# The feed-forward part of a decoder step: 18 seven-product tiles that add in PSUM, with down products between their blocks

## The chip, the cores and the metric

The kernel runs on one core of a Trainium2 chip. The metric is the device time of one execution in microseconds, from the runs shown below. Engines are called PE or TensorE (matmuls; PEld is its weight load), DVE or VectorE, ACT or ScalarE, POOL or GpSimd, and SP (the queue that issues most of the loads).

## The reference

One layer of a decoder trunk, for 512 prompt tokens and 8 sample tokens that share the weights (520 columns in all), D = 1024, feed-forward width 2816, all float32. The edit concerns its last part:

```
h2 = RMSNorm(x) * (1 + scale2) + shift2
gu, up = split(h2 @ w_ffn_in)            # 1024 -> 2 x 2816
x = x + gate2 * ((silu(gu) * up) @ w_ffn_out)   # 2816 -> 1024
y = RMSNorm(x)
```

Ahead of it stand adaLN, the input projection, an RG-LRU branch, an attention branch (prompt, and sample tokens with a paged cache) and the projection of their sum; none of that is touched.

## The kernel before, in words

Activations are kept transposed: features on the 128 partitions, the 520 tokens along the free axis, in two halves of 260 (`L_`, `R_`). Products of float32 are made of three fast ones: each operand is split into a high part (`hi`, an ACT cast) and a low rest (`lo`, a VectorE difference), and the matmuls are hi x hi, lo x hi, hi x lo. So one product of a 128x128 weight tile with half the tokens is three matmuls of 128x260. A weight tile of the common kind is split by L226 (ACT, `whi`) and L228 (VectorE, `wlo`).

The feed-forward part works through 22 tiles `jt` of 128 features. A tile is made in one of two ways.

- A plain tile (`ffn_tile`): gate (`fig`) and up (`fiu`) each need 8 weight tiles x 2 halves x 3 = 48 matmuls, 96 in all.
- A seven-product tile (`fast_tile`, the tiles in `FAST`): gate and up are taken as one 2x2 block product, of weight halves by token halves, with seven block products instead of eight (A11, A12, S2, S3, S1, A22, S4); a block is 4 weight tiles x 3 = 12 matmuls, 84 in all. The weight blocks S1 to S4 are sums and differences of raw weights that POOL makes (`ws`, L241 to L244). Each block's weights are split by L248 (ACT) and L249 (VectorE) into a `wb` tile. Each block product has a PSUM bank of its own. VectorE adds the seven into four results in SBUF (L1565, seven sums), ACT takes Silu of the gate, VectorE multiplies (L1568) and the result is split into `ach` (ACT, L1435) and `acl` (VectorE, L1436).

Tiles 0 and 1 are done by halves in a loop of their own, 2 and 3 are plain. The 22 tiles stand in four sections (`SECT`: 6, 6, 5, 5 tiles). At the end of a section its down products follow: for each of the 8 output tiles a `product` over the section's tiles (`fo`), and `residual` adds it to `x`, times the gate, on VectorE (L1392 for the left half; L1396, L1399 and L1400 for the right half and its 8 sample columns). The last section's down products go by halves (`by_halves`), since the sum of squares for the final norm is made beside them, on POOL for the first outputs; the outputs of the left half follow on POOL (L1518) during the right half.

Order: each engine works through its own queue. Weights are handled as a list of `units`, one for each stretch of matmuls; `begin` starts a unit, asks for the loads of units up to 22 us ahead (`load_chunks`, on SP) and for the splits of units up to 11 us ahead (`split_upto`). The split weights live in two rings of three buffers (`whi`, `wlo`); a block uses one buffer of either, a common weight tile one of each. Raw weights live in `wraw`, two buffers of 1 MB; `pg` is another pool of seven buffers. PSUM has eight banks, and 60 buffers in `heap` hold everything of 520 columns. The lines above are those of the profile.

Of the kernel before, what the change touches and what calls it, by code (L numbers as in the profile page):

```python
# [8 lines left out]
F32 = mybir.dt.float32  # L9
# [10 lines left out]
NS = 8  # L20
# [3 lines left out]
FF = 2816  # L24
# [40 lines left out]
def kernel(ctx, tc, xT, par, gates, b_f, cst, cse, own, cache_k, cache_v, cache_lf, pt,  # L65
# [76 lines left out]
    SECT = ((0, 6), (6, 12), (12, 17), (17, 22))  # L142
    PLAIN = 2
    CH_FI = len(chunks)
    for j0, j1 in SECT:
        for jt in range(j0, j1):
            chunks.append(cols(w_fi, 128 * jt, 128) + cols(w_fi, FF + 128 * jt, 128))
        for i in range(0, KT, 2):
            chunks.append(cols(w_fo, 128 * i, 256, 128 * j0, j1 - j0))


    FAST = (4, 5, 6, 7, 9, 10, 12, 13, 15, 16, 17, 18, 20)
    BLOCKS = ("A11", "A12", "S2", "S3", "S1", "A22", "S4")
    units = []
    for c, parts in enumerate(chunks):
        nk = parts[0][2]
        if parts[0][0] is w_fi and parts[0][3] // 128 in FAST:
            units += [(c, name, 4) for name in BLOCKS]
            continue
        for o in range(0, sum(p[4] for p in parts), 128):  # L160
            units.append((c, o, nk))
# [43 lines left out]
    def split_upto(n):  # L205
        while state["split"] < len(units) and state["split"] <= n:
# [5 lines left out]
            if isinstance(o, str):  # L212
                splits[m] = split_block(raw, o)
                continue
# [20 lines left out]
    def split_block(raw, name):  # L235
# [9 lines left out]
        src = blocks[name]  # L245
# [1144 lines left out]
    def residual(f, ps, gate, j):  # L1390
# [4 lines left out]
        n = NP - HALF  # L1395
        dve.scalar_tensor_tensor(x[f][:, HALF:NP], ps[:, :n], mod[:, gate, f, 0:1], x[f][:, HALF:NP],  # L1396
                                 ALU.mult, ALU.add)
        t = small("rs", 128, NS)
        dve.tensor_tensor(t, ps[:, n:HALF], mod[:, gate, f, 1:9], ALU.mult)  # L1399
# [163 lines left out]
    def fast_tile(jt):  # L1563
        t, v, w, out = slot("sw"), slot("v"), slot("w"), pair_out()
        add = lambda o_, a_, b_: dve.tensor_tensor(o_, b_, a_, ALU.add)  # L1565

        def close(j, part):
            dve.tensor_tensor(t[:, part], t[:, part], w[:, part], ALU.mult)  # L1568
            split_part(out, t[:, part], part)

        for name in BLOCKS:
            n = begin()
            b = bank(f"fi{jt}_{name}")[:, :HALF]
            hi, lo = splits[n]
            for k in range(4):
                ah, al = h2_block(name, k)
                for m, (wt, at) in enumerate(((hi, ah), (lo, ah), (hi, al))):
                    state["mm"] = pe.matmul(b, lhsT=wt[k], rhs=at, start=k == 0 and m == 0, stop=k == 3 and m == 2)  # L1578
            if name == "A11":
                act.copy(w[:, R_], b)  # L1580
            elif name == "A12":
                add(t[:, L_], w[:, R_], b)
                act.activation(t[:, L_], t[:, L_], AF.Silu)
            elif name == "S2":
                add(v[:, L_], w[:, R_], b)
            elif name == "S3":
                add(w[:, L_], v[:, L_], b)
            elif name == "S1":
                add(w[:, R_], w[:, L_], b)
                add(v[:, R_], v[:, L_], b)  # L1590
            elif name == "A22":
                add(w[:, L_], w[:, L_], b)
                close(0, L_)
            else:
                add(t[:, R_], v[:, R_], b)
                act.activation(t[:, R_], t[:, R_], AF.Silu)
                close(1, R_)
            run_later(n)
        return out

    for sec, (j0, j1) in enumerate(SECT):
        ac = []
        if j0 == 0:
            ts = [slot("sw") for _ in range(PLAIN)]
            ready = []
            u = state["n"]
            for j in range(2):
                for m in range(2 * PLAIN):
                    if j == 0:
                        begin(u + 3)  # L1610
                    b = bank(f"fi{m}_{j}")
                    half_product(u + m, j, h2, b)
                    ready.append((times_up if m % 2 else swish, b, ts[m // 2], j))
                    if j == 0 and m == 0:
                        rstd_half("r2", ss2, r2, 1)
                    if j or m:
                        for fn, *args in ready:
                            fn(*args)
                        ready.clear()
                    if j == 0 and m == 0:  # L1620
                        h2_half(1)
                    first = u + 2 * PLAIN
                    if j == 0:
                        load_chunks(units[first + m][0])
                    elif m:
                        split_upto(first + m - 1)
            for t in ts:
                out = pair_out()
                split_part(out, t)
                ac.append(out)  # L1630
        for jt in range(max(j0, PLAIN), j1):
            if jt == PLAIN:
                for k in range(4):
                    h2_blocks(k)
                defer(0, lambda: split_blocks(0))
# [71 lines left out]
```

## Time and profile before

| | |
|---|---|
| time, median of 3 runs | 1046.94 us (1045.0 to 1053.59) |
| profiled execution | 1044.21 us, span of its instructions 1042.3 us |
| PE busy | 998.9 us (96%), 8054 instructions |
| DVE busy | 777.5 us (75%) |
| ACT busy | 533.2 us (51%) |
| POOL busy | 304.0 us (29%) |
| granted TensorE clock, mean | 0.991 |
| chain that ended last | PE 70%, DVE 12%, DMA 7%, ACT 5% |

The feed-forward part fills the time from about 660 us to the end. A busy share is a mean over all stages; the chain of work that ended last, read in order of time, says for each stage which engine the others wait for. Rows of the group view give line, engine, operation, out<-in and shapes, then busy us, mean ns of one, and the idle time of the engine before them with what ended it.

### The profile page before, as it was taken

Reading aid. Unit: us, or ns where it says so; the run is one execution under the profiler, and the core shown is the slowest. Engines: PE = TensorE matmul, PEld = TensorE weight load, DVE = VectorE, ACT = ScalarE, POOL = GpSimd, SP = SyncE. Lnnn points to the kernel's source line nnn. Section 1 sums busy time; section 2 is a strip of 40 time slices with the busy share of each in tenths; the row PEclk is TensorE's granted clock in tenths of the full one; section 3 lists DMA queues with packets and bytes.
Section 4 is the critical chain, followed back from the end, with each engine's and each line's share of the span. In section 5 each row is a group of like instructions: output and inputs, shape, how many; then the busy total and the mean of one; then the engine's idle time right before and its main releaser. Section 6 shows DMA issues by size and latency. Waiting matters only on the chain.

```text
span 1042.3 us, 21246 instructions
## 1 busy us (share of the span) xinstructions
PE 998.9 (96%) x8054; PEld 925.8 (89%) x8054; DVE 777.5 (75%) x1370; ACT 533.2 (51%) x1072; POOL 304.0 (29%) x411
## 2 busy tenths in 40 slices
PE   4999999999999999999999999899999999999993
PEld 1888899999898988878888989899999999999993
DVE  5447999988989978886665546778589558869663
ACT  4523665857671467767793234555244324524451
POOL 0224411112133235654500003472224033223113
PEclk9999999999999999999999999999999999999997
DMA  9898987787889999996766863132343234143212
GB/s 326 295 306 289 300 281 216 262 253 270 263 253 309 321 326 284 303 274 213 263 230 209 282 226 82 41 82 75 100 111 83 91 111 121 54 128 102 75 52 83
DMA packets 165353, 206.97 MB, mean 199 GB/s; under 512 B 9842, under 2 KB 126082, under 8 KB 165186
## 3 DMA queue, kind: packets, MB, share of 16 engines
q1 hardware_dynamic: 148530, 152.52, 47.2%
q0 software_dynamic: 13040, 46.67, 13.5%
q10 hardware_dynamic: 3680, 6.42, 1.7%
q8 instruction: 63, 1.03, 0.4%
q14 instruction: 40, 0.33, 0.1%
HBM read 192.49 MB, written 13.09 MB: 197 GB/s over the span
## 4 chain that ended last, share of the span: by engine, by line
PE 70%; DVE 12%; DMA 7%; ACT 5%; issue 4%; POOL 1%; SPq 0%; POOLq 0%; DVEq 0%; ACTq 0%
PE fo L281 11%; PE fi_S L1578 7%; PE fi_A L1578 5%; PE pb L281 4%; PE gb L281 4%; PE fig L281 4%; PE fiu L281 4%; PE ga L281 3%; PE k L281 3%; PE wo L281 3%; PE v L281 3%; DVE wlo L228 2%; PE gr L281 2%; PE xr L281 2%; DMA wraw<-in_w_in_dram 2%
## 5 line engine op out<-in xcount | busy, mean ns | idle before, releaser
L226 ACT CAST whi<-wraw 128x1024 fp32r<-128x1024 f32 (+2 forms) x113 | 111.4, 987 | 186.1 <-PE fo L281 45.0
L228 DVE TENSOR_TENSOR wlo<-wraw,whi 128x1024 fp32r<-128x1024 f32 (+2 forms) x113 | 137.3, 1216 | 48.6 <-ACT whi L226 40.9
L281 PE MATMUL fo<-ach,whi 128*128 128x260 f32 x302 | 85.6, 283 | 0.0
L281 PE MATMUL fo<-ach,wlo 128*128 128x260 f32 x302 | 85.2, 282 | 0.0
L281 PE MATMUL fo<-acl,whi 128*128 128x260 f32 x302 | 85.0, 282 | 0.0
L658 POOL DMA_DIRECT2D pg<-in_cache_k_dram x74 | 39.4, 533 | 142.4 <-DVE S L707 70.5
L241 POOL TENSOR_TENSOR ws<-wraw 128x512 f32<-128x512 f32 x13 | 20.0, 1538 | 193.5 <-DMA wraw<-in_w_fi_dram 188.7
L706 DVE TENSOR_TENSOR pg<-pg,qb 128x1024 f32<-128x1024 f32 x48 | 58.0, 1227 | 2.4 <-DMA pg<-in_cache_k_dram 2.4
L707 DVE TENSOR_REDUCE S<-pg 128x16 f32<-128x1024 f32 x48 | 57.0, 1207 | 0.1
L281 PEld LDWEIGHTS fo<-ach,whi 128*128 128x128 f32 x302 | 56.8, 188 | 0.2
L281 PEld LDWEIGHTS fo<-ach,wlo 128*128 128x128 f32 x302 | 56.8, 188 | 0.0
L281 PEld LDWEIGHTS fo<-acl,whi 128*128 128x128 f32 x302 | 56.8, 188 | 0.0
L1191 POOL TENSOR_SCALAR p<-p,mu 128x128 f32<-128x128 f32 (+3 forms) x28 | 35.9, 1293 | 48.2 <-DVE mu L1187 31.6
L249 DVE TENSOR_TENSOR wb<-ws,wb 128x512 fp32r<-128x512 f32 x52 | 45.8, 891 | 4.2 <-ACT wb L248 4.1
L373 POOL TENSOR_TENSOR ss<-ss,sq 128x260 f32<-128x260 f32 x18 | 13.7, 761 | 111.3 <-PE ada L344 58.9
L248 ACT CAST wb<-ws 128x512 fp32r<-128x512 f32 x52 | 31.5, 619 | 26.2 <-PE fi_S L1578 8.6
L1185 ACT ACTIVATE p<-p,mu 128x128 f32<-128x128 f32 (+3 forms) x64 | 35.3, 552 | 15.8 <-DVE mu L1184 15.5
L248 ACT CAST wb<-wraw 128x512 fp32r<-128x512 f32 x39 | 23.9, 620 | 34.7 <-PE fo L281 18.1
L1396 DVE SCALAR_TENSOR_TENSOR x<-fo,mod,x 128x252 f32<-128x252 f32 x32 | 15.2, 477 | 32.4 <-PE fo L281 32.4
L1435 ACT CAST ach<-sw 128x260 fp32r<-128x260 f32 (+1 forms) x42 | 17.6, 419 | 41.5 <-DVE sw L1477 22.3
L281 PE MATMUL v<-hh,whi 128*128 128x260 f32 x128 | 37.3, 291 | 1.1 <-DVE pl L1205 1.1
L1578 PE MATMUL fi_S<-twh,wb 128*128 128x260 f32 x208 | 38.1, 282 | 0.0
(435 smaller groups left out, 4065.7 us busy)
## 6 DMA issues: line engine op xcount, KB each, us to landing
araw<-in_ada_w_dram SPq DMA_DIRECT2D x48, 512.0 KB, 6.2
wraw<-in_w_fi_dram SPq DMA_DIRECT2D x44, 512.0 KB, 5.2
pg<-in_cache_k_dram POOLq DMA_DIRECT2D x42, 512.0 KB, 6.2
pg<-in_cache_v_dram SPq DMA_DIRECT2D x42, 512.0 KB, 5.5
wraw<-in_w_in_dram SPq DMA_DIRECT2D x34, 512.0 KB, 7.7
wraw<-in_w_in_dram SPq DMA_DIRECT2D x11, 1024.0 KB, 10.3
pg<-in_cache_v_dram POOLq DMA_DIRECT2D x22, 512.0 KB, 6.4
pg<-in_cache_k_dram POOLq DMA_DIRECT2D x32, 256.0 KB, 5.7
```

Source lines behind the costliest of these rows:

```text
L226: state["act"] = act.copy(hi[:, :k1 - k0], src)
L228: state["last"] = dve.tensor_tensor(lo[:, :k1 - k0], src, hi[:, :k1 - k0].bitcast(F32), ALU.subtract)
L241: pool.tensor_tensor(s1, a21, a22, ALU.add)
L248: state["act"] = act.copy(t[:, :4], src)
L249: state["last"] = dve.tensor_tensor(t[:, 4:], src, t[:, :4].bitcast(F32), ALU.subtract)
L281: state["mm"] = pe.matmul(out[:, :HALF], lhsT=wt[k], rhs=at, start=k == 0 and m == 0, stop=k == nk - 1 and m == 2)
L658: done.append(eng.dma_start(pg, cache[bass.ds(r, 1), :, c0:c1].rearrange("a p c -> (a p) c")))
L706: dve.tensor_tensor(pg, pg, q, ALU.mult)
L707: last = dve.tensor_reduce(S[r // 2][:, c:c + H], pg.rearrange("p (h d) -> p h d", d=DH), AX.X, ALU.add)
L1185: act.activation(p[:, :n + 128], p[:, :n + 128], AF.Exp, bias=mu[:, 0:1], scale=-1.0, accum_out=mu[:, 1:2])
L1191: (pool.tensor_scalar(p, p, mu[:, 2:3], None, ALU.mult) if a and i + 1 < KT else act.activation(p, p, AF.Copy, scale=mu[:, 2:3]))
L1578: state["mm"] = pe.matmul(b, lhsT=wt[k], rhs=at, start=k == 0 and m == 0, stop=k == 3 and m == 2)
```

## The change

Sections are gone. All tiles from 4 to 21 are seven-product tiles (18 instead of 13; 8, 11, 14, 19 and 21 are new). The order of blocks is A11, S2, S3, S1, A12, A22, S4, and four PSUM banks X, Y, W, Z hold a tile's results from first block to last: A12 goes on adding into X, A22 into W, S4 into Z, where VectorE has put the sums of the others (four sums instead of seven; some of them read a bank and write a bank). Product and split read the bank.

Down products come in groups of four tiles, and the last of six (tiles 16 to 21). Group g (tiles 4g to 4g+3) is worked off in the next tiles, one down product behind block S2 and one behind block A12 (`JOIN`): two in each of tiles 4 to 16 and 21, one (behind A12) in each of 17 to 20. Their weights are four tiles deep, so they are split as a block is (`split_four`, L272 and L273 in the new numbering), into one `wb` buffer, and their raw weights are loaded into the `pg` pool instead of `wraw`. The last group goes by halves as before. In `residual` the product for the 8 sample columns (`rs`) now stands ahead of the wide one.

```diff
-    SECT = ((0, 6), (6, 12), (12, 17), (17, 22))
+    GROUP = 4
     PLAIN = 2
+    LAST = 16
+    JOIN = {}
+    for jt in range(GROUP, LAST):
+        JOIN[jt] = {"S2": (jt // GROUP - 1, 2 * (jt % GROUP)), "A12": (jt // GROUP - 1, 2 * (jt % GROUP) + 1)}
+    for i, (jt, name) in enumerate(((16, "S2"), (16, "A12"), (17, "A12"), (18, "A12"), (19, "A12"), (20, "A12"),
+                                    (21, "S2"), (21, "A12"))):
+        JOIN.setdefault(jt, {})[name] = (LAST // GROUP - 1, i)
-    FAST = (4, 5, 6, 7, 9, 10, 12, 13, 15, 16, 17, 18, 20)
-    BLOCKS = ("A11", "A12", "S2", "S3", "S1", "A22", "S4")
+    BLOCKS = ("A11", "S2", "S3", "S1", "A12", "A22", "S4")
...
+        for name in BLOCKS:
+            units.append((c, name, 4))
+            if name in JOIN[jt]:
+                g, i = JOIN[jt][name]
+                if i % 2 == 0:
+                    joined.add(len(chunks))
+                    chunks.append(cols(w_fo, 128 * i, 256, 128 * GROUP * g, GROUP))
+                units.append((max(joined), 128 * (i % 2), GROUP))
...
-            raw = wp.tile([128, KT, 256], F32, name="wraw", tag="wraw", bufs=2)
+            if c in joined:
+                raw = pgp.tile([128, GROUP, 256], F32, name="wraw", tag="pg")
+            else:
+                raw = wp.tile([128, KT, 256], F32, name="wraw", tag="wraw", bufs=2)
...
+            if c in joined:
+                splits[m] = split_four(raw[:, :, o:o + 128])
+                continue
...
+        t = small("rs", 128, NS)
+        dve.tensor_tensor(t, ps[:, n:HALF], mod[:, gate, f, 1:9], ALU.mult)
         dve.scalar_tensor_tensor(x[f][:, HALF:NP], ps[:, :n], mod[:, gate, f, 0:1], x[f][:, HALF:NP],
                                  ALU.mult, ALU.add)
-        t = small("rs", 128, NS)
-        dve.tensor_tensor(t, ps[:, n:HALF], mod[:, gate, f, 1:9], ALU.mult)
...
-    def fast_tile(jt):
-        t, v, w, out = slot("sw"), slot("v"), slot("w"), pair_out()
+    def fast_tile(jt, ac):
+        sw, cp, u2, out = slot("sw"), slot("cp"), slot("u2", HALF), pair_out()
+        X, Y, W, Z = (bank(f"fi{jt}{n}")[:, :HALF] for n in "xywz")
+        into = {"A11": X, "S2": Y, "S3": W, "S1": Z, "A12": X, "A22": W, "S4": Z}
...
+        def close(b, part):
+            dve.tensor_tensor(b, b, sw[:, part], ALU.mult)
+            split_part(out, b, part)
...
             if name == "A11":
-                act.copy(w[:, R_], b)
+                act.copy(cp[:, L_], X)
+            elif name == "S2":
+                add(u2, cp[:, L_], Y)
+            elif name == "S3":
+                add(W, u2, W)
+            elif name == "S1":
+                act.copy(cp[:, R_], Z)
+                add(Z, u2, Z)
+                add(Y, cp[:, R_], W)
             elif name == "A12":
...
+                act.activation(sw[:, L_], X, AF.Silu)
             elif name == "A22":
+                close(W, L_)
+            elif name == "S4":
+                act.activation(sw[:, R_], Z, AF.Silu)
+                close(Y, R_)
             run_later(n)
+            if name in JOIN[jt]:
+                g, i = JOIN[jt][name]
+                product(f"fo{g}_{i}", ac[GROUP * g:GROUP * g + GROUP], lambda j, b_, i=i: residual(i, b_, 5, j))
```

What stands on VectorE in tile 4 before, from the first sum to the first product (`fi4_A12` and the like are the banks of the blocks, `w` and `v` buffers in SBUF, `wb` a split of block weights):

```order
L1565 TENSOR_TENSOR sw_10292<-fi4_A12_10319,w_10294 128x260
L249 TENSOR_TENSOR wb_10233<-wraw_10066,wb_10233 128x512
L1565 TENSOR_TENSOR v_10293<-fi4_S2_10337,w_10294 128x260
L249 TENSOR_TENSOR wb_10299<-wraw_10066,wb_10299 128x512
L1565 TENSOR_TENSOR w_10294<-fi4_S3_10354,v_10293 128x260
L249 TENSOR_TENSOR wb_10316<-ws_10227,wb_10316 128x512
L1565 TENSOR_TENSOR w_10294<-fi4_S1_10371,w_10294 128x260
L1565 TENSOR_TENSOR v_10293<-fi4_S1_10371,v_10293 128x260
L249 TENSOR_TENSOR wb_10334<-ws_10228,wb_10334 128x512
L1565 TENSOR_TENSOR w_10294<-fi4_A22_10389,w_10294 128x260
L1568 TENSOR_TENSOR sw_10292<-sw_10292,w_10294 128x260
```

And with the change, on VectorE in tile 9, from the sum behind S2 to the one behind S1 (`fi9y` is bank Y of tile 9, `cp` and `u2` are in SBUF, `fo1_2` is group 1's down product for output tile 2, `x` the residual stream):

```order
L1591 TENSOR_TENSOR u2_11321<-fi9y_11325,cp_11320 128x260
L273 TENSOR_TENSOR wb_11344<-wraw_11020,wb_11344 128x512
L1416 SCALAR_TENSOR_TENSOR x_8863<-fo1_2_0_11372,mod_102,x_8863 128x260
L1421 TENSOR_TENSOR rs_11399<-fo1_2_1_11386,mod_102 128x8
L1422 SCALAR_TENSOR_TENSOR x_8863<-fo1_2_1_11386,mod_102,x_8863 128x252
L1424 TENSOR_TENSOR x_8863<-x_8863,rs_11399 128x8
L273 TENSOR_TENSOR wb_11360<-ws_11157,wb_11360 128x512
L1591 TENSOR_TENSOR fi9w_11326<-fi9w_11326,u2_11321 128x260
L273 TENSOR_TENSOR wb_11369<-wraw_11227,wb_11369 128x512
L273 TENSOR_TENSOR wb_11403<-ws_11363,wb_11403 128x512
L1591 TENSOR_TENSOR fi9z_11327<-fi9z_11327,u2_11321 128x260
L1591 TENSOR_TENSOR fi9y_11325<-fi9w_11326,cp_11320 128x260
```

Residuals stand between splits and sums, three sums write a PSUM bank, and the splits are for weights of five or six units later.

On PE, with the change, the rows with a wait from the last down product of tile 9 to the first one of tile 10 (`[waits ...]` names the engines whose semaphores the row waits for; `wb` is its weight):

```order
L305 MATMUL fo1_3_1_11473<-ach_10285,wb_11328 128x260 [waits DVE_49]
...
L1603 MATMUL fi9w_11326<-tuh_10052,wb_11344 128x260 [waits DVE_49,Activation_49]
...
L1603 MATMUL fi9z_11327<-h2h_9396,wb_11360 128x260 [waits Activation_49]
...
L1603 MATMUL fi10x_11531<-h2h_9370,wb_11369 128x260 [waits Activation_49]
...
L1603 MATMUL fi10y_11532<-twh_10056,wb_11403 128x260 [waits Activation_49]
...
L305 MATMUL fo1_4_0_11579<-ach_10285,wb_11437 128x260 [waits Activation_49]
L305 MATMUL fo1_4_0_11579<-ach_10285,wb_11437 128x260 [waits DVE_49]
```

The `fi9w` row is block A22; its wait for DVE is the one for the sum into bank Y (the last row of the fence before), which reads W. The wait of `fi10y`, the second block of tile 10, is for the ACT cast of its weight. Before, all seven blocks of a tile were first writers of a bank, and no block of a tile waited for a sum of that tile.

More of the change, by code (lines that the diff above doesn't have):

```diff
@@ L1598, in fast_tile @@
             run_later(n)
-        return out
[L1601 to L1635, printed above, removed]
-                defer(1, lambda: split_blocks(2))
-            ac.append((fast_tile if jt in FAST else ffn_tile)(jt))
-        if j1 == FF // 128:
-            tail += [slot("ss3"), slot("r3")]
-            by_halves("fo", ac, fo_done, fo_between)
-            fo_between(1)
-        else:
-            for i in range(KT):
-                product(f"fo{sec}_{i}", ac, lambda j, b: residual(i, b, 5, j))
```

89 lines of the change are left out of this document (55 added, 34 removed).

## The prediction

> **What bounds the kernel now.** I read the page first, for the share of each engine, then the chain in order of time for the feed-forward part (where the whole edit lies), then the waits of TensorE (PE), then the costs of the instructions on VectorE (DVE) that the edit adds or drops, and last the end of the program.
>
> ```profile
> PE 998.9 (96%) x8054; PEld 925.8 (89%) x8054; DVE 777.5 (75%) x1370; ACT 533.2 (51%) x1072; POOL 304.0 (29%) x411
> ```
>
> That share is a mean over stages. In the feed-forward part itself the chain is TensorE alone. These rows are start, length, what:
>
> ```profile
> 708.75 2.87 PE fi_A L1578 x24
> ...
> 728.90 34.50 PE fo L281 x288
> ...
> 773.49 2.87 PE fi_A L1578 x24
> 776.36 4.32 PE fi_S L1578 x36
> 780.68 1.45 PE fi_A L1578 x12
> 782.13 1.44 PE fi_S L1578 x12
> 783.57 5.74 PE fig L281 x48
> 789.31 5.74 PE fiu L281 x48
> ```
>
> The first row is where tile 4 starts. Each piece starts where the one before ends. A matmul costs 34.50 / 288 = 0.120 us, whichever product it belongs to. A seven-product tile is 84 matmuls and 2.87 + 4.32 + 1.45 + 1.44 = 10.08 us; a plain tile (gate and up) is 96 and 11.48 us. All that TensorE waited for between 640 us and the end (total, times, longest):
>
> ```profile
> PE r L380 <- DVE ss L373: 2.2, 1, 2.2
> PE fi L281 <- DVE h2l L1431: 1.1, 3, 0.5
> ```
>
> The rest of that list belongs to the closing norm. Both rows lie ahead of tile 2, in code that stays. So from tile 2 to the last down product only fewer matmuls help, and only a new wait of TensorE hurts.
>
> VectorE is the engine that could make such a wait. Two stretches, two seven-product tiles and the plain tile behind them (columns: the stretch, its length, busy us and instructions of PE, PEld, DVE, ACT, POOL, clock, DMA share, GB/s):
>
> ```profile
> 763.40:783.60 20.20, 20.20 (x171) 20.20 (x170) 17.47 (x34) 11.19 (x20) 4.19 (x4) 1.00 0.40 105
> 783.60:795.00 11.40, 11.40 (x97) 11.40 (x96) 10.51 (x11) 3.77 (x10) 9.76 (x7) 1.00 0.34 93
> ```
>
> In the first VectorE needs 0.51 us an instruction; in the second, where GpSimd (POOL) is busy for 9.76 us, 0.96 us. TensorE loses nothing in either, since weights are split up to six units ahead. The clock is 1.00 in both.
>
> **The change part by part.**
>
> *Five plain tiles become seven-product tiles* (8, 11, 14, 19, 21). TensorE drops 12 matmuls in each: 5 x (11.48 - 10.08) = 7.0 us (60 x 0.120 = 7.2 us by the other row). The 1056 down matmuls stay 1056, in groups of 4, 4, 4, 4, 6 tiles instead of 6, 6, 5, 5. Nothing hides this gain, because TensorE is the chain there: -7.0 us.
>
> *VectorE's work a tile.* Its rows (busy, mean ns; for the first row the spread):
>
> ```profile
> L249 DVE TENSOR_TENSOR wb<-ws,wb x52: 675/692/1792, 704.1 to 975.7; 128x512 fp32r<-128x512 f32 x52
> ...
> L249 DVE TENSOR_TENSOR wb<-ws,wb 128x512 fp32r<-128x512 f32 x52 | 45.8, 891 | 4.2 <-ACT wb L248 4.1
> L1436 DVE TENSOR_TENSOR acl<-sw,ach 128x260 fp32r<-128x260 f32 x39 | 20.9, 536 | 6.2 <-ACT ach L1435 6.2
> L1392 DVE SCALAR_TENSOR_TENSOR x<-fo,mod,x 128x260 f32<-128x260 f32 x32 | 15.5, 485 | 5.6 <-PE fo L281 5.5
> L1396 DVE SCALAR_TENSOR_TENSOR x<-fo,mod,x 128x252 f32<-128x252 f32 x32 | 15.2, 477 | 32.4 <-PE fo L281 32.4
> L1568 DVE TENSOR_TENSOR sw<-sw,w 128x260 f32<-128x260 f32 x26 | 14.3, 550 | 0.3
> L1400 DVE TENSOR_TENSOR x<-x,rs 128x8 f32<-128x8 f32 x32 | 12.5, 391 | 0.8
> L1565 DVE TENSOR_TENSOR w<-fi_S,w 128x260 f32<-128x260 f32 x13 | 5.5, 427 | 3.2 <-PE fi_S L1578 3.0
> L1399 DVE TENSOR_TENSOR rs<-fo,mod 128x8 f32<-128x8 f32 x32 | 4.9, 153 | 0.0
> ```
>
> A tile with two down products gets 132 matmuls, 15.8 us, and on VectorE nine splits (9 x 0.89 = 8.0 us), four sums instead of seven (1.7), two products (1.1), two differences (1.1) and two residuals of 0.485 + 0.477 + 0.153 + 0.391 = 1.5 each (3.0): 14.9 us. A tile with one down product (17 to 20) has 108 matmuls, 12.9 us, against 8 x 0.89 + 1.7 + 1.1 + 1.1 + 1.5 = 12.5 us. The same sum for a tile of before is 7 x 0.89 + 7 x 0.43 + 1.1 + 1.1 = 11.4 us against 10.08, and two of those in a row stalled nothing. So VectorE stays below TensorE, by 6% and 3%; the splits ahead of time take up what is uneven. Bounds: if every split fell beside GpSimd's work, at up to 1.79, it could not keep up (first rival); if products and differences cost 0.43 it has 0.5 us more room. I take no stall.
>
> Four of these results are new kinds: sums, products and differences that read a PSUM bank and write it, or keep it. No row has a sum written to PSUM; the nearest is the reciprocal, with PSUM output and without:
>
> ```profile
> L1512 DVE RECIPROCAL r3p<-r 128x260 f32<-128x260 f32 x1 | 1.8, 1786 | 1.8 <-ACT r L1510 1.8
> L382 DVE RECIPROCAL r<-r 128x260 f32<-128x260 f32 x1 | 1.8, 1768 | 0.0
> ```
>
> 1% apart, so I price them as 0.43. The rows also say which of them suffer beside GpSimd: L1565, with one operand in PSUM, has a mean of 427 ns, L1568 and L1436, with both in SBUF, 550 and 536. The Trainium skill (SBUF — State Buffer, section Who interferes with whom) states this as a rule: a VectorE instruction with two SBUF inputs contends with a GpSimd instruction that reads SBUF, one with at most one does not. The rows agree; by the rule the four closing instructions cost 0.43 and a tile's sum is 14.4 instead of 14.9 us.
>
> *New waits of TensorE.* Block A22 now adds into bank W, which two sums have read and written first. From the end of S1: an ACT split, a VectorE split, sums Z and Y. With
>
> ```profile
> L248 ACT CAST wb<-ws 128x512 fp32r<-128x512 f32 x52 | 31.5, 619 | 26.2 <-PE fi_S L1578 8.6
> L1435 ACT CAST ach<-sw 128x260 fp32r<-128x260 f32 x39 | 16.0, 409 | 34.1 <-DVE sw L1568 19.2 <-DVE sw L1477 14.9
> L243 POOL TENSOR_TENSOR ws<-wraw 128x512 f32<-128x512 f32 x12 | 20.3, 1694 | 0.0
> ```
>
> that is 0.62 + 0.69 (1.79) + 0.86 = 2.2 to 3.3 us; A12 and a down product, 36 matmuls, cover 4.3 us. Cost 0; without the down product there the cover would be 1.4 us and the wait 0.8 to 1.9. At tiles 8, 12 and 16 the first down product reads the tile just closed: ACT split 0.62, VectorE split 0.69 to 1.79, product 0.43, split again, ACT cast 0.41, difference 0.43 to 0.54, so 3.3 to 5.6 us, against two blocks and 21 matmuls of the product, 45 x 0.120 = 5.4 us. Cost 0 to 0.2 us, three times; I take 0.2 in all. ACT has nine splits and six 260-wide instructions a tile, 9 x 0.62 + 6 x 0.41 = 8.0 of 15.8 us. GpSimd gets four more instructions in each of five tiles, 5 x 4 x 1.7 = 34 us, beside TensorE's work, never on its path.
>
> *The loads.* Down weights come in 20 loads instead of 16, into another pool; two of them stand in SP's queue ahead of the weights of tiles 5 and 6 and wait for GpSimd's block differences, the last of which was
>
> ```profile
> 689.23 1.21 POOL L1549 TENSOR_TENSOR u<-h2r,w 128x260 f32<-128x260 f32 x1
> ...
> wraw<-in_w_fo_dram SPq DMA_DIRECT2D x4, 768.0 KB, 4.4
> ```
>
> done at 690.4. A load lands in 4.4 us and is asked for 22 us ahead, and tile 5 starts 15.8 us behind tile 4's 708.75. Cost 0. Were the cover gone, each would show as a wait of up to 4.4 us.
>
> *The end.* In the last section each product has 18 matmuls instead of 15. Before, the chain there left TensorE:
>
> ```profile
> 1015.83 5.68 POOL L1518 TENSOR_TENSOR y<-x,r 128x260 f32<-128x260 f32 x8 [9.79 <-DVE rs L1399]
> 1021.44 3.22 POOL L373 TENSOR_TENSOR ss<-ss,sq 128x260 f32<-128x260 f32 x4
> ...
> 1024.09 0.28 PE L281 MATMUL fo<-acl,whs 128*128 128x260 f32 x1
> ...
> 1024.70 0.43 DVE L373 TENSOR_TENSOR ss<-ss,sq 128x260 f32<-128x260 f32 x1 [3.11 <-POOL ss L373]
> ...
> 1025.71 0.47 DVE L1396 SCALAR_TENSOR_TENSOR x<-fo,mod,x 128x252 f32<-128x252 f32 x1
> ...
> 1026.29 0.17 DVE L1400 TENSOR_TENSOR x<-x,rs 128x8 f32<-128x8 f32 x1
> ```
>
> GpSimd did eight outputs and then four sums until 1024.66; VectorE's sum waited for it, and the last two residuals stood behind that sum, so the last one began 1.34 us after the last matmul (1024.37). In the change the second pass lasts 8 x 18 x 0.120 = 17.3 instead of 14.4 us, while GpSimd's outputs begin only one product's growth (0.36 us) later against its start. So against the last matmul GpSimd is done 2.9 - 0.36 = 2.5 us earlier, which is more than the 1.34 us that it was late. The last residual then starts 0.1 us (an estimate) after the last matmul: 1.2 us less. The new order of the residual (rs first) moves nothing more there. Bounds 0 and -1.3; I take -1.2, since the pass grows by more than the lateness.
>
> **Sum**: -7.0 - 1.2 + 0.2 = -8.0 us on the profiled execution's 1044.21: 1036.2. The runs shown lie higher, 1045.0 the lowest and 1046.94 the median; by the lowest I add 0.8: **1037.0 us**.
>
> **The rivals.**
>
> *VectorE becomes the bound* (the other side). Place: tiles 4 to 21; price: if the 6.8 us of GpSimd work in each tile (four of L243's length) meet four splits at 1.79, a two-product tile needs 4 x 1.79 + 5 x 0.69 + 6.9 = 17.5 us, 1.7 more than TensorE; a one-product tile 4 x 1.79 + 4 x 0.69 + 5.4 = 15.3, 2.4 more. 14 x 1.7 + 4 x 2.4 = 33 us, 1070. It decides from 15.8 us a tile. For it: splits at 1.79 exist, and GpSimd now works in every tile. Against: the mean is 0.89 with GpSimd as busy, and starts in a row overlap. Half of it gives 1053.
>
> *PSUM held too long.* Four banks stay taken through a tile. If the second block of the next tile had to wait for the closing of bank Y (ACT split 0.62, Silu 0.41, product 0.43, cast 0.41, difference 0.43, one split 0.69: 3.0 us against one block of 1.44), each of 17 changes of tile would cost 1.6 us, 27 us in all: 1064. Against it: eight banks, and in the built order that block waits for its weights alone. The Trainium skill (PSUM — Partial Sum Buffer, Summary: rules for kernel authors) speaks for this rival: "Evacuate promptly — 2 MiB is tight."
>
> *The gain is taken back by late weights.* Weights of S2 are wanted one block sooner, behind the same two GpSimd results: one block, 1.44 us, lost in five tiles gives back the 7.0, 1044. Against: raw weights are asked for 22 us ahead, a tile is 10 to 16.
>
> **How the numbers follow.** Forecast 0.74, with 1035.5 to 1040 of its own (tail -1.3 or 0, offset to the runs 0 to 2.7); VectorE 0.09, half of it beyond 1057; PSUM 0.07; late weights 0.10. A measurement here tells about 1% from no change, so faster means below 1036.5: 0.4 of the forecast, 0.30. Slower means above 1057.4: half of VectorE's and PSUM's share, 0.12. The rest, 0.58, is within 1%. Range 1034 to 1047: the low end is the forecast's, with 1.5 us for the scatter of runs, the high end takes in late weights and leaves out most of the two slow rivals.
>
> **What would show it.** Right: 60 fewer matmuls; the chain from tile 4 on in unbroken TensorE pieces, a seven-product tile with its two down products 15.8 us long; no wait of TensorE on bank Y or W worth a microsecond; VectorE below 95% in 20 us stretches; GpSimd's last sums done before the last matmul. Wrong: TensorE rows that wait for L1591 or L1460 results, or for wb from L273; splits with a mean above 1.1 us; a time above 1047.

## The result, and the profile after

| | before | after |
| --- | --- | --- |
| runs, median (lowest to highest), us | 1047.24 (1045.0 to 1053.59, 6 runs) | 1037.79 (1036.26 to 1039.79, 6 runs) |
| ratio after / before, 95% interval | | 0.9894 (0.987 to 0.9919) |
| profiled execution: time / span, us | 1044.21 / 1042.3 | 1036.26 / 1034.6 |
| tile 4's first matmul starts, us | 708.58 | 710.07 |
| from there to the end of the last down matmul, us | 315.79 | 308.07 |
| from there to the end, us | 17.88 | 16.47 |

The ratio is the one on record, and not the quotient of the two medians, which is 0.991. The change is faster by about 1%: the whole interval lies below 1, and all six runs after lie below the lowest before. By the medians it is 9.5 us, by the profiled spans 7.7 us.

The three lower rows split the profiled execution: ahead of tile 4, from tile 4 to the last down matmul, and the end. "The stretch" below is the middle one. (Where an expectation has 17.93 us for the end, it is taken from a span rounded to 0.1 us; the trace has 17.88.) These are its first rows in the timeline of TensorE, before and after, and its last one after (start, length, engine, line, instruction):

```profile
708.58 0.39 PE L1578 MATMUL fi_A<-h2h,wb 128*128 128x260 f32 x2
```

```profile
710.07 0.39 PE L1603 MATMUL fi4x<-h2h,wb 128*128 128x260 f32 x2
...
1017.86 0.28 PE L305 MATMUL fo<-acl,whs 128*128 128x260 f32 x1
```

The engines' row of the page after, and all that TensorE waited for from 640 us to the end:

```profile
PE 993.8 (96%) x7994; PEld 920.1 (89%) x7994; DVE 795.3 (77%) x1416; ACT 549.4 (53%) x1128; POOL 333.9 (32%) x431
```

```profile
PE r L404 <- DVE ss L397: 1.4, 1, 1.4
PE fi L305 <- DVE h2l L1455: 1.1, 3, 0.4
PE r L1533 <- ACT sq L1514: 0.3, 1, 0.3
```

There are 60 matmuls fewer. The first two waits lie ahead of tile 2 and the third in the closing norm: no wait stands between. Such a list leaves out idle times under 0.15 us, and it counts from the modelled end of a matmul, 0.28 us after its start, though matmuls follow each other every 0.12 us. So each wait in it is about 0.16 us short of what it cost, and the length of the stretch is the finer measure. The chain through tile 9, with its two down products:

```profile
789.17 1.44 PE fi9x L1603 x12
790.61 1.43 PE fi9y L1603 x12
792.05 2.86 PE fo L305 x24
794.91 1.43 PE fi9w L1603 x12
796.34 1.44 PE fi9z L1603 x12
797.78 1.44 PE fi9x L1603 x12
799.21 2.87 PE fo L305 x24
802.08 1.44 PE fi9w L1603 x12
803.52 1.43 PE fi9z L1603 x12
```

Each piece starts where the last one ends: 15.8 us for the tile. VectorE beside it, in 16 us of two-product tiles and 13 us of one-product tiles (columns as in the prediction: stretch, length, busy us of PE, PEld, DVE, ACT, POOL):

```profile
788.00:804.00 16.00, 16.00 (x136) 16.00 (x136) 13.30 (x26) 7.55 (x16) 6.29 (x5) 1.00 0.35 99
942.00:955.00 13.00, 13.00 (x111) 13.00 (x110) 11.70 (x21) 6.90 (x15) 5.32 (x5) 1.00 0.30 82
```

VectorE is busy for 83% and 90% of these. In stretches of 20 us from 710 to 990 us it is busy for at most 17.86 us (89%), and its block weight splits have means of 0.87 and 0.94 us. The prediction's signs were 95% and 1.1 us. At the end, the timeline shows GpSimd's eight outputs and four sums, then VectorE's sum and its last residual:

```profile
1005.66 5.66 POOL L1542 TENSOR_TENSOR y<-x,r 128x260 f32<-128x260 f32 x8 [9.49 <-DVE rs L1421]
...
1011.29 3.23 POOL L397 TENSOR_TENSOR ss<-ss,sq 128x260 f32<-128x260 f32 x4
...
1015.10 0.43 DVE L397 TENSOR_TENSOR ss<-ss,sq 128x260 f32<-128x260 f32 x1 [0.56 <-ACT sq L396]
...
1018.18 0.17 DVE L1421 TENSOR_TENSOR rs<-fo,mod 128x8 f32<-128x8 f32 x1 [1.52 <-PE fo L305]
```

GpSimd is done at 1014.52, 3.6 us ahead of the end of the last matmul (1018.14), and VectorE's sum now waits for ScalarE's square. The last residual waits for the last matmul alone and starts 0.04 us behind it, where it was 1.34 us.

### The profile page after: what moved, and what is told of

Read it like the earlier page. It is cut to its first block, busy times and chain, and to the rows that moved or that the text cites. A ratio compares the mean times of both kernels' runs of the same rounds, so it can differ in the third digit from the quotient of the medians.

```text
span 1034.6 us, 21301 instructions
## 1 busy us (share of the span) xinstructions
PE 993.8 (96%) x7994; PEld 920.1 (89%) x7994; DVE 795.3 (77%) x1416; ACT 549.4 (53%) x1128; POOL 333.9 (32%) x431
## 4 chain that ended last, share of the span: by engine, by line
PE 70%; DVE 12%; DMA 6%; ACT 4%; issue 4%; POOL 2%; SPq 1%; POOLq 0%; ACTq 0%; DVEq 0%
PE fo L305 9%; PE pb L305 4%; PE gb L305 4%; PE xr L305 3%; PE ga L305 3%; PE k L305 3%; PE wo L305 3%; PE v L305 3%; DVE wlo L250 2%; PE gr L305 2%; PE qp L527 2%; DVE pg L730 2%; PE pv L815 2%; PE po L1258 2%; PE ada L368 1%
## 5 line engine op out<-in xcount | busy, mean ns | idle before, releaser
L248 ACT CAST whi<-wraw 128x1024 fp32r<-128x1024 f32 (+1 forms) x79 | 82.0, 1039 | 117.9 <-PE pb L305 35.0
L250 DVE TENSOR_TENSOR wlo<-wraw,whi 128x1024 fp32r<-128x1024 f32 (+1 forms) x79 | 101.3, 1284 | 30.1 <-ACT whi L248 25.9
L305 PE MATMUL fo<-ach,wb 128*128 128x260 f32 x512 | 93.3, 282 | 0.0
L272 ACT CAST wb<-ws 128x512 fp32r<-128x512 f32 x72 | 44.8, 622 | 91.2 <-PE fo L305 63.6
L305 PEld LDWEIGHTS fo<-ach,wb 128*128 128x128 f32 x512 | 78.8, 188 | 0.0
L273 DVE TENSOR_TENSOR wb<-ws,wb 128x512 fp32r<-128x512 f32 x72 | 67.5, 937 | 14.6 <-ACT wb L272 12.6
L273 DVE TENSOR_TENSOR wb<-wraw,wb 128x512 fp32r<-128x512 f32 x86 | 74.2, 863 | 5.1 <-ACT wb L272 4.4
L305 PE MATMUL fo<-acl,wb 128*128 128x260 f32 x256 | 72.3, 282 | 0.0
L272 ACT CAST wb<-wraw 128x512 fp32r<-128x512 f32 x86 | 53.6, 623 | 33.6 <-ACT cp L1612 5.8
L305 PEld LDWEIGHTS fo<-acl,wb 128*128 128x128 f32 x256 | 48.1, 188 | 0.0
L305 PE MATMUL ga<-hh,wlo 128*128 128x260 f32 x128 | 36.9, 288 | 0.9 <-DVE wlo L250 0.9
L305 PE MATMUL k<-hh,whi 128*128 128x260 f32 x128 | 37.3, 291 | 0.0
L305 PE MATMUL ga<-hh,whi 128*128 128x260 f32 x128 | 37.0, 289 | 0.0
```

The lines of the kernel that those rows point to most:

```text
L248: state["act"] = act.copy(hi[:, :k1 - k0], src)
L250: state["last"] = dve.tensor_tensor(lo[:, :k1 - k0], src, hi[:, :k1 - k0].bitcast(F32), ALU.subtract)
L272: state["act"] = act.copy(t[:, :4], src)
L273: state["last"] = dve.tensor_tensor(t[:, 4:], src, t[:, :4].bitcast(F32), ALU.subtract)
L305: state["mm"] = pe.matmul(out[:, :HALF], lhsT=wt[k], rhs=at, start=k == 0 and m == 0, stop=k == nk - 1 and m == 2)
```

## The experiments

All are compared by the stretch of their profiled execution and by the time behind it, since the start of tile 4 differs from run to run by more than most of these effects (last section).

| kernel | stretch, us | behind it, us | ratio to before, 95% interval |
| --- | --- | --- | --- |
| before | 315.79 | 17.88 | |
| change | 308.07 | 16.47 | 0.9894 (0.987 to 0.9919) |
| e1 before, last group of six | 315.77 | 16.60 | 0.9991 (0.9971 to 1.0012) |
| e2 before, all tiles seven-product | 319.53 | 17.98 | 1.0033 (1.0015 to 1.0051) |
| e3 change, five plain tiles | 315.30 | 16.47 | 0.9973 (0.9952 to 0.9993) |
| e4 change, A22 without cover | 327.55 | 16.46 | 1.0051 (1.0033 to 1.0069) |
| e5 change, sums in SBUF | 308.55 | 16.46 | 0.9888 (0.9848 to 0.9928) |
| e6 change, two splits more a tile | 308.48 | 16.46 | one run, 1039.38 us |
| e7 change, four splits more a tile | 315.28 | 16.46 | one run, 1045.94 us |
| e8 change, tile 3 seven-product | 322.95 from tile 3 on | 16.45 | 0.9952 (0.9932 to 0.9971) |
| e11 change, half the look-ahead | 309.05 | 16.46 | one run, 1039.69 us |
| e12 change, five banks | 308.07 | 16.45 | one run, 1039.94 us |

**e1: the last group of six alone.**

```diff
-    SECT = ((0, 6), (6, 12), (12, 17), (17, 22))
+    SECT = ((0, 6), (6, 11), (11, 16), (16, 22))
```

> Kernel before with the last group of six tiles instead of five (groups of 6, 5, 5, 6); nothing else. The same 8054 matmuls. Theory (the tail gains because GpSimd is done before the last matmul): time from the last down matmul to the end 17.93 -> about 16.6 us, GpSimd's four sums end before the last matmul, the whole is 1.2 to 1.5 us shorter. Rival (the tail is shorter in the change because of the new order of the residual, or by chance): the tail stays at 17.9 us, the whole is unchanged.

The stretch is the same, and the end is 1.28 us shorter, 16.60, as the theory had it. In its timeline GpSimd's sums end ahead of VectorE's sum, which no longer waits for them:

```profile
1025.47 3.22 POOL L373 TENSOR_TENSOR ss<-ss,sq 128x260 f32<-128x260 f32 x4
...
1029.38 0.43 DVE L373 TENSOR_TENSOR ss<-ss,sq 128x260 f32<-128x260 f32 x1 [0.56 <-ACT sq L372]
```

The runs of the whole kernel can't tell so small a gain from nothing (their interval holds 1). This kernel has the old order of the residual, so `rs` first is worth at most the 0.13 us by which the end of the change is shorter still.

**e2: seven-product tiles without the rest of the change.**

```diff
-    FAST = (4, 5, 6, 7, 9, 10, 12, 13, 15, 16, 17, 18, 20)
+    FAST = tuple(range(4, 22))
```

> Kernel before with every tile from 4 on as a seven-product tile of its own old kind (seven banks, sums in SBUF, down products in one stretch behind each section). 60 matmuls fewer, as in the change. Theory A (only the number of matmuls counts; VectorE keeps up, since it was busy 17.47 of 20.20 us in two such tiles in a row): -7.0 to -7.2 us against before. Theory B (summed durations count: 11.4 us of VectorE's work in a tile of 10.08 us, in runs of 2 to 6 tiles, with the splits ahead as the only buffer): TensorE loses up to 1.3 us a tile, 18 x 1.3 = 23 us, so between -7 and +16 us, with waits of TensorE on wb in the list of waits. If A holds, the placing of the down products and the sums in PSUM brought nothing of the gain.

Theory A fell: there are 60 matmuls fewer, and the stretch is 3.7 us longer. Against the 7.2 us of those matmuls, 11.0 us are lost. The waits of TensorE from 700 us on, without the two of the closing norm, and two stretches of 20 us in the second group of tiles:

```profile
PE fi_A L1578 <- DVE wb L249: 3.5, 4, 1.4
PE fi_S L1578 <- DVE wb L249: 2.9, 4, 1.3
PE fo L281 <- ACT ach L1435: 0.7, 1, 0.7
```

```profile
780.00:800.00 20.00, 20.00 (x168) 20.00 (x167) 19.93 (x31) 9.23 (x20) 8.94 (x7) 1.00 0.39 105
800.00:820.00 20.00, 16.92 (x135) 16.09 (x134) 19.85 (x32) 10.18 (x22) 9.08 (x7) 1.00 0.33 93
```

VectorE is busy without a pause. In the first 20 us TensorE still runs on the splits made ahead; in the second it stands for 3.1 us and waits for weights (wb). VectorE's rows there, at times with GpSimd at work (796.87 to 803.14 and from 807.82 us on) and without it, show what GpSimd costs:

```profile
801.92 1.50 DVE L1568 TENSOR_TENSOR sw<-sw,w 128x260 f32<-128x260 f32 x1
...
803.95 0.42 DVE L1436 TENSOR_TENSOR acl<-sw,ach 128x260 fp32r<-128x260 f32 x1
...
809.58 0.41 DVE L1565 TENSOR_TENSOR w<-fi_A,w 128x260 f32<-128x260 f32 x1
810.03 1.07 DVE L1568 TENSOR_TENSOR sw<-sw,w 128x260 f32<-128x260 f32 x1
```

Beside GpSimd the product (L1568), with both operands in SBUF, takes 1.50 and 1.07 us. The difference (L1436), also with both in SBUF, takes 0.42 us while GpSimd stands still, and the sum (L1565), with one operand in PSUM, takes 0.41 us beside GpSimd. This is theory B, at about half its price: 11.0 us lost instead of 23.

**e3: the rest of the change without the seven-product tiles.** Tiles 8, 11, 14, 19, 21 are plain again; a down product stands behind gate and one behind up (one product in tile 19).

```diff
+    KEEP = (8, 11, 14, 19, 21)
...
-        for name in BLOCKS:
-            units.append((c, name, 4))
+        for name in ("S2", "A12") if jt in KEEP else BLOCKS:
+            units.append((c, 128 * (name == "A12"), KT) if jt in KEEP else (c, name, 4))
...
-        ac.append(fast_tile(jt, ac) if jt >= GROUP else ffn_tile(jt))
+        ac.append(ffn_tile(jt, ac) if jt < GROUP or jt in KEEP else fast_tile(jt, ac))
```

> The changed kernel with tiles 8, 11, 14, 19 and 21 as plain tiles again (gate, up), the down products behind gate and behind up there. 60 matmuls more than the change. Theory (matmul count): +7.0 us (60 x 0.120 = 7.2) against the change, and a chain of TensorE without gaps. Rival (VectorE or the banks hold TensorE a little in the change, hidden in the pieces): less than +5 us, since plain tiles give VectorE room.

308.07 + 7.23 = 315.30: these are the 60 matmuls at 0.120 us, and the list of waits has nothing in the tiles. The rival fell. With e2, all four combinations of the two parts of the change have been run: neither 315.79; the tiles alone 319.53; the rest alone 315.30; both 308.07. The rest alone gains 0.5 us, the tiles alone lose 3.7 us, and together they gain 7.7 us.

**e4: A22's cover taken away.** The second down product goes from behind A12 to behind S3.

```diff
-        JOIN[jt] = {"S2": (jt // GROUP - 1, 2 * (jt % GROUP)), "A12": (jt // GROUP - 1, 2 * (jt % GROUP) + 1)}
+        JOIN[jt] = {"S2": (jt // GROUP - 1, 2 * (jt % GROUP)), "S3": (jt // GROUP - 1, 2 * (jt % GROUP) + 1)}
```

(and "S3" for "A12" in the list for tiles 16 to 21)

> The changed kernel with the second down product of each tile moved from behind A12 to behind S3, so that only A12 (12 matmuls, 1.44 us) stands between S1 and A22; the number of matmuls is the same. Theory (A22 waits for the two sums that read bank W; in the change they end 2.14 us after S1's last matmul, and by the bounds 2.2 to 3.3 us): 0.7 to 1.9 us a tile, 18 tiles with A12 alone ahead of A22, +13 to +34 us against the change, shown as waits of TensorE on a DVE result of the sums' line. Rival (the sums come earlier once the down product's residuals stand elsewhere, or the wait is not on the path): within 2 us of the change.

The stretch is 19.5 us longer, 1.08 us a tile, as the theory had it. In tile 9 S1's last matmul starts at 806.33. VectorE's rows, then TensorE's:

```profile
807.35 1.57 DVE L273 TENSOR_TENSOR wb<-wraw,wb 128x512 fp32r<-128x512 f32 x1
808.84 0.42 DVE L1591 TENSOR_TENSOR fi9z<-fi9z,u 128x260 f32<-128x260 f32 x1
809.18 0.42 DVE L1591 TENSOR_TENSOR fi9y<-fi9w,cp 128x260 f32<-128x260 f32 x1
```

```profile
807.89 0.40 PE L1603 MATMUL fi10x<-h2h,wb 128*128 128x260 f32 x2
...
809.32 0.51 PE L1603 MATMUL fi9z<-h2h,wb 128*128 128x260 f32 x2 [0.79 <-DVE fi9z L1591]
809.67 0.28 PE L1603 MATMUL fi9z<-h2l,wb 128*128 128x260 f32 x1
809.78 0.40 PE L1603 MATMUL fi9w<-tuh,wb 128*128 128x260 f32 x2
```

The two sums end 3.0 us behind S1 (806.61 to 809.60), held up by a split of 1.57 us. A22 (fi9w) starts 1.9 us behind A12, which ends where fi10x starts. The order that the scheduler built fills part of that with four matmuls of the next tile's A11 and three of S4, and the rest is idle. So in the change the down product is what hides this wait. (In the change the sums end 2.1 us behind S1. There the split ahead of them took 0.69 us; here it ran beside GpSimd, so part of the 1.9 us comes from that and not from the shorter cover.)

**e5: sums in SBUF, the down products still between the blocks.** fast_tile joins seven banks as before, blocks in the old order, products behind S2 and S1.

```diff
-    BLOCKS = ("A11", "S2", "S3", "S1", "A12", "A22", "S4")
+    BLOCKS = ("A11", "A12", "S2", "S3", "S1", "A22", "S4")
...
-        X, Y, W, Z = (bank(f"fi{jt}{n}")[:, :HALF] for n in "xywz")
...
+            b = bank(f"fi{jt}_{name}")[:, :HALF]
```

> The changed kernel with the old way of joining the blocks: seven banks, seven sums into SBUF, blocks in the order A11, A12, S2, S3, S1, A22, S4; the down products stay between the blocks (behind S2 and S1). The matmuls are those of the change. It adds three sums a tile on VectorE, and puts both operands of products and differences into SBUF. Theory A (what counts is that VectorE's busy time in a tile, 13.3 to 13.8 us in 16 us, stays below TensorE's): 13.5 + 1.3 to 1.6 = at most 15.1 of 15.8 us, and 12.7 to 13.0 of 12.95 in tiles with one product: 0 to +1 us against the change from tile 4 to the last matmul (307.9 us there). So interleaving alone brings the gain. Theory B (the sum of durations counts): 14.9 + 1.3 = 16.2 of 15.8 us, 13.8 of 12.9: +9 us. That would show that the sums in PSUM were needed too.

The stretch is 0.5 us longer, as theory A had it. The same two windows as after:

```profile
788.00:804.00 16.00, 16.00 (x136) 16.00 (x135) 14.57 (x30) 7.12 (x14) 5.81 (x5) 1.00 0.36 99
942.00:955.00 13.00, 13.00 (x110) 13.00 (x109) 13.00 (x23) 6.30 (x13) 5.27 (x5) 1.00 0.31 84
```

VectorE needs 1.3 us more in each and is busy for all of a one-product tile, and the list of waits still has nothing in the tiles. So the sums in PSUM are not what brings the gain: they bring 1.3 us of room on VectorE and half a microsecond of time. Against e2, which joins its blocks in the same way, e5 has the down products between the blocks, and with that their groups of four, their own loads and their split into `wb` buffers. Over the whole stretch VectorE is even busier in e5 than in e2, 273.0 us against 268.0, and e2 loses 11.0 us while e5 loses nothing to waits: what counts is when VectorE's work falls due, not how much it is. The place and its companions were not run apart.

**e6 and e7: how much room.** Splits that VectorE does twice:

```diff
-        return split_four(blocks[name])
+        return split_four(blocks[name], name in ('S2', 'A12'))
...
-        state["last"] = dve.tensor_tensor(t[:, 4:], src, t[:, :4].bitcast(F32), ALU.subtract)
+        for _ in range(1 + twice):
+            state["last"] = dve.tensor_tensor(t[:, 4:], src, t[:, :4].bitcast(F32), ALU.subtract)
```

(e7: 'S2', 'S1', 'A12', 'S4')

> The changed kernel in which VectorE does the weight split of blocks S2 and A12 twice in every seven-product tile (the second writes the same values again): 1.4 to 1.9 us more of VectorE a tile. Theory A (busy time): 13.5 + 1.9 = 15.4 of 15.8 us, 12.8 to 13.3 of 12.95: 0 to +1.5 us on the 307.9 us from tile 4 to the last matmul. Theory B (sum of durations, the first rival's rule): 14.9 + 1.8 = 16.7 of 15.8, 14.3 of 12.95: 14 x 0.9 + 4 x 1.4 = +18 us.

> The same with four splits done twice (S2, S1, A12, S4): 2.8 to 3.8 us more of VectorE a tile. Theory A: 16.3 to 17.3 us against 15.8, and 14.2 to 15.2 against 12.95: 14 x (0.5 to 1.5) + 4 x (1.2 to 2.2) = +12 to +30 us, VectorE near 100% busy. Theory B: 18.5 against 15.8 and 16.1 against 12.95: +50 us.

Two splits more cost 0.4 us. The list of TensorE's matmuls has no wait, but that of its weight loads has one, for the sums ahead of A22 in tile 18 (`PEld fi18w L1604 <- DVE fi18y L1592: 0.3, 1, 0.3`). Four splits more cost 7.2 us, below theory A's range. All waits of TensorE in e7 from 700 us to 1020, and its windows:

```profile
PE fi17w L1604 <- DVE fi17y L1592: 1.7, 1, 1.7
PE fi19w L1604 <- DVE fi19y L1592: 1.4, 1, 1.4
PE fi18w L1604 <- DVE fi18y L1592: 1.3, 1, 1.3
PE fi20w L1604 <- DVE fi20y L1592: 0.9, 1, 0.9
```

```profile
788.00:804.00 16.00, 16.00 (x136) 16.00 (x135) 15.88 (x30) 7.38 (x15) 6.41 (x4) 1.00 0.37 104
942.00:955.00 13.00, 11.73 (x98) 11.53 (x97) 12.97 (x23) 4.51 (x11) 6.42 (x4) 1.00 0.38 107
```

Only the one-product tiles break, 17 to 20. The two-product tiles take four splits more, with VectorE busy for 15.88 of 16.00 us, and no wait of theirs stands in the list. Theory A's rule held, but its sum for these tiles (16.3 to 17.3) was too high. And where VectorE breaks first is A22's wait for the sums, not the weights.

**e8: tile 3 as well.**

```diff
-    JOIN = {}
+    JOIN = {GROUP - 1: {}}
...
-        if jt < GROUP:
+        if jt < GROUP - 1:
...
-        ac.append(fast_tile(jt, ac) if jt >= GROUP else ffn_tile(jt))
+        ac.append(fast_tile(jt, ac) if jt >= GROUP - 1 else ffn_tile(jt))
```

> The changed kernel with tile 3 as a seven-product tile too (no down product in it): 12 matmuls fewer. Theory (GpSimd is done with the block inputs at 690 us, tile 3 begins near 699 us; its first two block differences take 2 x 1.7 us and the split 1.3 us, so S2 is ready at 695): 1.4 us less, span 1033.2 on the profiled execution's terms. Rival (GpSimd, still at the block inputs, makes S2 or S3 of tile 3 late): a wait of TensorE in tile 3 of up to 3 us, and no gain.

There is no gain but a loss. From tile 3's first matmul (701.40) to the last down matmul it took 322.95 us, where 308.07 + 10.08 = 318.15 were to be had: 4.8 us are lost, more than the 1.4 that the tile saves. Tile 3 also began 2.8 us later than in the change (710.07 - 11.48 = 698.6). Of this, 1.3 us stand in the list as longer waits for `h2l` ahead of tile 2 (2.4 us, where the change, e3, e5 and e12 have 1.1); the rest one execution can't tell from scatter. The waits from tile 3 on, the window around the first, and a split ahead of it:

```profile
PE fi3y L1603 <- DVE twl L339: 2.2, 3, 1.1
PE fo L305 <- DVE acl L1460: 0.6, 2, 0.4
```

```profile
701.40:708.90 7.50, 5.53 (x41) 4.81 (x39) 7.50 (x15) 4.76 (x10) 0.00 (x0) 1.00 0.08 23
```

```profile
699.88 1.78 DVE L339 TENSOR_TENSOR tul<-u,tuh 128x520 fp32r<-128x520 f32 x1
```

The place was the rival's, the mechanism another. TensorE waits not for GpSimd's differences but for VectorE, which is busy for 7.50 of 7.50 us with the splits of the block inputs, with work of tile 2 and weight splits among them. GpSimd has a share in that lateness: its four block sums and differences ran from 695.13 to 701.10, and the split beside them took 1.78 us, where those behind them took 0.68.

**e9, e10, e12: fewer PSUM banks.** Banks are allocated at tile 4 and read behind tile 21. In e9 and e10 that reading hung on nothing late, and the scheduler put it at 707 to 710 us, ahead of tile 4's first matmul, so that nothing was held: they show only the change again (308.07 us each). e12 ties it to tile 21's result:

```diff
+    holds = []
     for jt in range(PLAIN, FF // 128):
+        if jt == GROUP:
+            holds += [bank(f"hold{i}") for i in range(3)]
+            for h_ in holds:
+                dve.tensor_copy(h_[:, :8], cs[:, :8])
...
+    for h_ in holds:
+        dve.tensor_tensor(small("hold", 128, 8), h_[:, :8], ac[-1][1][:, NT - 8:NT].bitcast(F32), ALU.add)
```

> The changed kernel with three of the eight PSUM banks kept from use from tile 4 to tile 21 (eight values are written to each ahead of tile 4 and read behind tile 21); five are left for the four sums and the down products. Theory (a bank is free soon enough; by the trace of the change at most five or six are in use at a time, and the sixth only for the last tenths of a microsecond): 0 to +6 us on the 307.9 us from tile 4 to the last matmul. Rival (PSUM held too long is close: the four sums and two halves of each product need nearly all eight): +27 us or more, shown as waits of TensorE on bank Y or on a residual.

> The same with four banks kept from use, four left. X, Y, W and Z take them all, so the second down product waits for the Silu that frees X (about 1 us) and its second half for the residual of its first (about 1 us). Theory: +2 to +3 us for each of 18 tiles, +36 to +54 us. If it is below +10, banks are of no weight at all here.

> The changed kernel with three of the eight PSUM banks held from tile 4 to the end of tile 21 (eight values are written to each ahead of tile 4, and read together with values of tile 21's result, so that they can't be read sooner); five are left for the four sums and the down products. Theory (a bank is free soon enough; by the trace of the change five or six are in use at a time, the sixth only for tenths of a microsecond, while X waits for its Silu and the product's second half begins): 0 to +6 us on the 308.07 us from tile 4's first matmul to the last. Rival (PSUM held too long is close: the four sums and two halves of each product need nearly all eight): +27 us or more, shown as waits of TensorE on bank Y or on a residual.

```profile
L1667 DVE TENSOR_TENSOR hold<-hold,acl x3: 156/156/157, 989.5 to 989.6; 128x8 f32<-128x8 f32 x3
```

The banks are held until 989.5 us, and the stretch is 308.07 us, to the hundredth that of the change. Five banks are enough. What four would cost stays open, since e10 held none.

**e11: half the look-ahead.**

```diff
+        if jt == GROUP:
+            state["lead"] = 5.5
```

> The changed kernel with half the look-ahead of the weight splits from tile 4 on (5.5 us of TensorE's work instead of 11, three to four units instead of six); loads as before. Theory (each tile has room on VectorE for its own work, 13.5 of 15.8 us): 0 to +3 us. Rival (late weights are close, and the look-ahead is what evens VectorE's 1.8 us splits beside GpSimd out): waits of TensorE on wb of 0.5 to 1 us a tile, +9 to +18 us.

The stretch is 1.0 us longer, within the theory's range. The list of TensorE's matmuls has no wait in it, but that of its weight loads does:

```profile
PEld fo L305 <- DVE wls L250: 0.6, 2, 0.3
```

These are late weights, at 992 and 997 us, in the down products of the last group (`wls` is the low part of their split). The gaps between matmuls above 0.135 us that the change doesn't have all lie from 991.9 to 999.7 us and add up to 1.0 us. In the tiles themselves half the look-ahead costs nothing.

## Why the prediction came out as it did

*The forecast's own terms.* Five tiles were to bring -7.0 us: e3 gives -7.23 for the same 60 matmuls. The rest of the change alone brings another -0.49 (before less e3), which has no term in the sum. The end, -1.2, was -1.41 in the change and -1.28 with the last group alone (e1), by the mechanism named. Only its size was off: against the last matmul GpSimd's sums end 3.9 us earlier than before instead of 2.5, but beyond the 1.34 us of lateness this brings nothing. Group boundaries were to cost 0.2; no wait stands there.

So the parts that the edit touches gained 9.1 us (7.72 + 1.41), where 8.0 were forecast. That the forecast still met the profiled execution (1036.2 to 1036.26) is luck: tile 4 began 1.49 us later there than in the profile before. That it came within 0.8 us of the median is in part luck too: the base that it was counted from, 1045.0, lay 2.2 us below the median of before (1047.24), and the gain by the medians was 9.5 us instead of 8.0.

*The step that was incomplete.* The prediction booked the gain to the tiles. It did work out that VectorE keeps up in the new order, but it gave the down products' new place no value: two such tiles in a row had stalled nothing before, at 11.4 us of VectorE's work against 10.08. e2 shows that this doesn't carry on over longer rows of such tiles. What kept the old kernel from stalling was the plain tile or the stretch of down products behind every two such tiles. With every tile of that kind and the old place of the down products, the first rival is what happens, and 11.0 us are lost. The place between the blocks turns 10.08 us of TensorE's work a tile into 15.8 or 12.95, and that makes the seven-product tiles pay.

*VectorE's sum.* 14.9 of 15.8 and 12.5 of 12.9 us were forecast; the windows show 13.30 of 16.00 and 11.70 of 13.00. Durations were added as if one instruction began where the last one ends. Added in that way, the rows of the first window make 14.6 us, and 14.4 for the 15.8 us of tile 9, which is the prediction's sum with 0.43 for the four closing instructions; the busy time is 1.3 us less, since instructions overlap. In the timeline of e2 two sums at 807.25 and 807.59 each last 0.42 us and start 0.34 apart. The first rival decides "from 15.8 us a tile", the prediction said: e7 bears the rule out with 15.88 of 16.00 us and no loss, and 12.97 of 13.00 with 1.3 us of TensorE lost. It needed four splits more. By the sum of durations e5 would already have stalled: its rows in the first window add up to 16.3 us in 16.00.

*A22's wait.* "Without the down product there the cover would be 1.4 us and the wait 0.8 to 1.9": e4 lost 1.08 a tile. The 2.2 to 3.3 us for the sums were 3.0 there in tile 9, and 2.1 in the change, so the mechanism and its size were right.

*PSUM held too long.* The second block of the next tile doesn't wait for the closing of bank Y. In the change, by the views of two tiles, it starts 1.5 us ahead of Y's last reading, in another bank:

```profile
L1603 PE MATMUL fi10y<-twh,wb x8: 280/282/283, 806.2 to 807.4; 128*128 128x260 f32 x8
```

```profile
L1460 DVE TENSOR_TENSOR acl<-fi9y,ach x1: 419/419/419, 807.7 to 807.7; 128x260 fp32r<-128x260 f32 x1
```

e12 takes three banks away at no cost. The rule in the Trainium skill (PSUM — Partial Sum Buffer, Summary: rules for kernel authors) that spoke for this rival has no price in this kernel with five to eight banks.

*Late weights.* There is no wait on `wb` in the change, and none in the tiles with half the look-ahead (e11), where 1.0 us of late weights appears in the last group alone. In e2 it is weights that come late, but because VectorE is full, not for the reason that this rival gave.

*Contention.* By the rule of the Trainium skill (SBUF — State Buffer, Who interferes with whom) the four closing instructions, with an operand in PSUM, do not contend with GpSimd; the prediction's second price for them, 0.43 us, is the one from the row of L1565. In the change the 36 products have a mean of 425 ns and the 36 differences of 417. With both operands in SBUF (e5) the products have a mean of 727 ns:

```profile
L1592 DVE TENSOR_TENSOR sw<-sw,w 128x260 f32<-128x260 f32 x36 | 26.2, 727 | 0.6
```

The measurement agrees with the rule, and the sum with 0.43 (14.4 us) was the right one of the two.

## What to carry to other kernels

When a faster form of a tile shifts work from the engine that sets the time to its helper, count the helper's work over as many such tiles in a row as the new order has, not over the two that the old profile shows. Work that falls nearly all to the engine that sets the time, such as products whose results the helper takes in with few instructions, is worth more between the new tiles than in a stretch of its own. Where a wait is hidden by one piece of work, take that piece away once: its price tells how near the edge the order stands.

## What was not expected of the hardware

The stretch from tile 4 to the last down matmul is the same to 0.01 us in the change, in e9 and e10, and in e12, which ran on another chip than these two (308.07), and to 0.02 us in before and e1. The scatter of the runs lies ahead of it: in the same kernels tile 4 begins at 708.58 (before) and 716.57 (e1), 710.07 (change) and 713.77 (e12). So half a microsecond could be told in one profile of a part, while the interval of whole runs is some 2.5 us on either side.

A VectorE that is busy 13.00 of 13.00 us (e5) made no wait in the list, and nor did 19.93 of 20.00 us in one window of e2, while in the next window 19.85 of 20.00 us went with 3.1 us lost: the busy share shows the edge, not the loss.
